# A two-layer fp32 decoder trunk: the seven-product results kept as one running sum in one PSUM bank, and two groups in every pair of the feed-forward's second part

## The chip, the cores and the metric

The kernel runs on one core of a Trainium2 chip. The metric is device time in microseconds (us) of one execution; less is better. Engines are named as in the profile: PE is TensorE (matmuls and transposes), PEld its weight loads, DVE is VectorE, ACT is ScalarE, POOL is GpSimd, SP the queue that issues most of the transfers.

## What is computed

Each of two layers runs a pre-normed mixer (a gated convolution branch beside forgetting attention), a SwiGLU feed-forward stage and a per-layer input embedding, all added onto x. There are 256 positions, 2048 model columns and 5632 hidden columns. The parts that the change touches are these products:

```
def rmsnorm(x, g):
    xf = x.astype(jnp.float32)
    y = xf * lax.rsqrt(jnp.mean(xf * xf, axis=-1, keepdims=True) + EPS)
    return (y * g.astype(jnp.float32)).astype(x.dtype)
...
    for i in range(DEPTH):
        h = rmsnorm(x, norm_mix_g[i])
        proj = h @ w_in[i]
        ...
        merged = jax.nn.sigmoid(g_conv) * y_conv + jax.nn.sigmoid(g_attn) * y_attn
        x = x + merged @ w_out[i]

        hf = rmsnorm(x, norm_ffn_g[i])
        gate, up = jnp.split(hf @ w_gate_up[i], 2, axis=-1)
        x = x + (jax.nn.silu(gate) * up) @ w_down[i]

        hp = rmsnorm(x, norm_ple_g[i])
        x = x + jax.nn.sigmoid(hp @ w_ple_gate[i]) * (p[i] @ w_ple_proj[i])
    return rmsnorm(x, final_g)
```

All weights are fp32, and every weight is read once from HBM.

## The kernel before

**Splits.** A weight piece is 128 partitions x 1024 numbers (two k-tiles of 128 rows, 512 columns each, 512 KB). `fetch` (L135) brings it on SP's queue into one of eight `raw` buffers. `split` (L138 to L144) makes two tensors of it that TensorE can take at full rate: `wh`, a rounded copy (ACT, L141), and `wl`, the rest `raw - wh` (DVE, L142), five buffers each. The operands on the activation side are split alike. A k-tile's product is then three matmuls of 512 columns, `xh*wh`, `xh*wl` and `xl*wh` (`Sum.add`, L184, L185, L186); a piece in the plain form is used for two blocks of 128 positions, so it takes 12 matmuls.

**The seven-product form.** `fast_chunks` (L233 to L310) makes two outputs of 512 columns, w1 and w2, over a list of groups of 512 rows of the weights. For the first groups, as many as `fast` holds, it takes the Strassen-Winograd form: the four quarter blocks of the pair of outputs come from seven products of six matmuls, 42 in place of 48. The operand side (B11 to N4X) is made once per group by `Fast.make` (L364 to L374): four small DVE sums on 128x256, then the splits (ACT L373, DVE L374). On the weight side a11, a12, a22 are pieces as fetched, and `sm` is w1 + w2, added while it lands by an accumulating transfer that POOL issues. Three DVE sums of 128x1024 per group (`add` L271, `sub` L272) make the other weight operands in place in the raw buffers. Before, four products add into banks of their own over all groups (`p1, q5, q6, q7`, tag ms, four banks of 512 columns in all, shared with the transposes), the other three straight into the output sums (tag mm). After the last group ACT copies p1 (L293) and DVE makes four sums of 128x512 with q6, q7 and twice q5 (L272, L271).

The remaining groups are plain: `go` fetches, splits and multiplies one piece. `u1` plus the first output's plain sum is the first result (`first(u1)`), `u2` is subtracted from the second output's plain sum at the end (the u2 subtraction, L272, whose operand is an mm bank).

**What sets the order.** Each engine has an in-order queue. A list scheduler puts the instructions into these queues, by data and by buffer dependences; the source order is what it starts from. Small work (transposes of finished operands, `turned` L334 with `halves` L321/L322 or `Fast.take`) hangs in a list and is released by `run()` calls between pieces. In a two-group call of `fast_chunks` before, `run()` is called only in the plain part that follows the groups; in a one-group call over eight plain tiles it is also called inside the group.

**Where it is called.** Twice two pairs for gates in the mixer, `w_out` (two pairs, one group in the first and two in the second), the feed-forward stage, and the per-layer embedding (PLE, one group in the first pair and two in the second). The feed-forward stage runs in three parts of 3, 4 and 4 hidden chunks (`FFN_PARTS`). A part first makes its hidden chunks, one gate/up pair per chunk c (operands `norm.fast`, L916 to L927: Silu on ACT, then two STT at L924 that multiply up by gate), then two pairs of the down product onto x (`residual` L881). The number of fast groups, nf, is 1 in the first pair of each and 2 in the others: `nf = 1 if c == c0 else 2` (gate/up), `nf = 1 if n == 0 else len(fast_hid)` (down). The PLE's pair ends in `embed` (sigmoid on ACT L963, two DVE instructions L965 and L966).

Of the kernel before, what the change touches and what calls it, by code (L numbers as in the profile page):

```python
# [13 lines left out]
ALU = mybir.AluOpType  # L14
# [31 lines left out]
def trunk(ctx, tc, xT, xR, pT, wI, wF, wC, wA, wOut, wGU, wD, wPG, wPP, vec, bF, gF, out):  # L46
# [124 lines left out]


    class Sum:
        def __init__(self, n, bank):
            self.n, self.left, self.bank = n, n, bank

        @property
        def t(self):
# [2 lines left out]
        def add(self, xh, xl, wh, wl):  # L181
            start = self.left == self.n
            self.left -= 1
            pe.matmul(self.t, lhsT=xh, rhs=wh, start=start, stop=False)  # L184
            pe.matmul(self.t, lhsT=xh, rhs=wl, start=False, stop=False)  # L185
            pe.matmul(self.t, lhsT=xl, rhs=wh, start=False, stop=self.left == 0)  # L186

    def once(make):

# [48 lines left out]
    def fast_chunks(fast, w1, w2, xs, ks, first, by_block=None):  # L238

        nf, nk = 2 * len(fast), 4 * len(ks)
        p1, q5, q6, q7 = (Sum(nf, once(bank_ms)) for _ in range(4))
        c1, c11, c12 = sums_of_blocks(nf + nk)
        c2, c21, c22 = sums_of_blocks(nf + nk, nk)
        if by_block is not None:
            c22 = Sum(nk, once(bank_ms))
        left = deque()
        for w, sums in ((w1, (c11, c12)), (w2, (c21, c22))):
            for g, k0 in enumerate(ks):  # L250
                for half in range(2):
                    left.append((w[len(fast) + g][:, half * 1024 : (half + 1) * 1024], sums, k0 + 2 * half))
        state = dict(quiet=True)

        def go(n=1):
            for _ in range(n):
                src, sums, k0 = left.popleft()
                parts = split(fetch(src))
                await_x(xs, (k0, k0 + 1))
                plain(sums, xs, k0, parts)  # L260
                if not state["quiet"]:
                    fill(CONV // 2 + len(left) % 2)
                    run()

        def product(to, operand, raw):
            h, l = split(raw)
            xh, xl = operand
            for kk in range(2):
                to.add(xh(kk), xl(kk), h[:, kk, :], l[:, kk, :])

        add = lambda o, a, b: dve.tensor_tensor(o, a, b, op=ALU.add)  # L271
        sub = lambda o, a, b: dve.tensor_tensor(o, a, b, op=ALU.subtract)  # L272
        u1, u2 = pair(), pair()
        for g, f in enumerate(fast):
            a11, sm = fetch(w1[g][:, :1024]), fetch(w2[g][:, :1024])
            nc.gpsimd.dma_start(sm.rearrange("p k n -> p (k n)"), w1[g][:, :1024], accum_op=ALU.add)
            a22, a12 = fetch(w2[g][:, 1024:]), fetch(w1[g][:, 1024:])
            product(p1, f(B11), a11)
            product(c21, f(N4X), a22)
            go()  # L280
            product(c11, f(B21), a12)
            if len(left) > 2 * len(ks):
                go()
            if nk == 8 and len(fast) == 1:
                run()
            product(q7, f(T3), sm)
            add(sm, sm, a22)
            product(q6, f(T2), sm)
            sub(a11, sm, a11)
            product(q5, f(M1), a11)  # L290
            add(a12, a12, sm)
            product(c12, f(B22), a12)
        act.activation(u1[:, 0, :], p1.t, AF.Copy)  # L293
        sub(u1[:, 1, :], u1[:, 0, :], q6.t)
        add(u2[:, 0, :], u1[:, 1, :], q7.t)
        add(u1[:, 1, :], u1[:, 1, :], q5.t)
        add(u2[:, 1, :], u2[:, 0, :], q5.t)
        state["quiet"] = False
        go(len(left) - 2 * len(ks))
        add(u1, u1, c1())  # L300
        first(u1)
        if by_block is None:
            go(len(left))
            sub(u2, c2(), u2)
            return u2
        go(len(left) - 4)
        held = [(split(fetch(src)), k0) for src, _, k0 in left]
        for b, c in enumerate((c21, c22)):
            for parts, k0 in held:
                plain([c, c], xs, k0, parts, [b])  # L310
            sub(u2[:, b, :], c.t, u2[:, b, :])
            by_block(b, u2)
# [25 lines left out]

        return (lambda b: o[:, b * P : (b + 1) * P]), (lambda b: o[:, S + b * P : S + (b + 1) * P])

    B11, B12, B21, B22, M1, T2, T3, N4X = range(8)

    class Fast:

# [17 lines left out]
        def make(self):  # L362
            f = lambda n: self.f[n // 4][:, n % 4]
            sub = lambda o, a, b, op: dve.tensor_tensor(f(o), f(a), f(b), op=op)  # L364
            sub(M1, B11, B12, ALU.subtract)
            sub(T2, M1, B22, ALU.add)
            sub(T3, B22, B12, ALU.subtract)
            sub(N4X, B21, T2, ALU.subtract)
            self.h, self.l = [], []
            for t in self.f:  # L370
                h, l = (pair(F32R).rearrange("p a b -> p (a b)") for _ in range(2))
                t = t.rearrange("p n k s -> p (n k s)")
                act.activation(h, t, AF.Copy)  # L373
                dve.tensor_tensor(l, t, h.bitcast(F32), op=ALU.subtract)  # L374
                self.h.append(h.rearrange("p (n k s) -> p n k s", n=4, k=2))
                self.l.append(l.rearrange("p (n k s) -> p n k s", n=4, k=2))
            self.f = None
# [167 lines left out]
    for i in range(L):  # L545
# [357 lines left out]
        for part, nch in enumerate(FFN_PARTS):  # L903
            hid = {}
            fast_hid = [Fast() for _ in range(nch - 2)]
            for c in range(c0, c0 + nch):
                w1, w2 = wGU[i, 2 * c], wGU[i, 2 * c + 1]
                o = pair() if c == 0 else None

                def gate(g):  # L910
                    nonlocal o
                    if o is None:
                        o = g
                    for b in range(2):
                        act.activation(o[:, b, :], g[:, b, :], AF.Silu, scale=norm.r(b))

                if c == 0:
                    gate(chunk(by_four(w1), norm.xs))
                    up = chunk(by_four(w2), norm.xs)
                else:  # L920
                    nf = 1 if c == c0 else 2
                    up = fast_chunks(norm.fast[:nf], w1, w2, norm.xs, range(4 * nf, KD, 4), gate)
                for b in range(2):
                    dve.scalar_tensor_tensor(  # L924
                        o[:, b, :], up[:, b, :], norm.r(b), o[:, b, :], op0=ALU.mult, op1=ALU.mult
                    )
                turns.append(  # L927
                    lambda c=c, o=o, hid=hid, fast=fast_hid[c - c0] if c - c0 < len(fast_hid) else None:
                    operand(hid, 4 * c, lambda b: o[:, b, :], fast)
                )  # L930
            for n in range(0, N4, 2):
                await_x(hid, (4 * c0,))
                on = after if part == len(FFN_PARTS) - 1 else None
                nf = 1 if n == 0 else len(fast_hid)
                onto_x(on, n + 1)(
                    fast_chunks(
                        fast_hid[:nf], wD[i, n][c0 : c0 + nch], wD[i, n + 1][c0 : c0 + nch], hid,
# [129 lines left out]
```

## Time and profile before

| | us |
|---|---|
| median of three runs (2793.18 to 2793.36) | 2793.24 |
| the profiled execution's own time | 2793.7 |
| its span | 2791.8 |

| engine | busy us | share of the span |
|---|---|---|
| PE | 2773.9 | 99% |
| PEld | 2293.5 | 82% |
| DVE | 2507.1 | 90% |
| ACT | 1660.0 | 59% |
| POOL | 79.4 | 3% |

The core moved 585.24 MB at 210 GB/s on average, and the granted clock was 0.999. The profile gives a row for each instruction with its start and its length. PE's rows overlap: a matmul's length is modelled and is longer than the distance to the next one, so what a matmul costs is read from the distance of two starts, and a real wait of PE shows as a greater distance. Rows of DVE overlap by some 80 ns too. "x8" behind a row says that eight equal ones follow each other; a name in brackets says who ended the idle time ahead of it.

### The profile page before, as it was taken

How to read it: one execution, taken by the hardware profiler on the slowest of the kernel's cores; microseconds unless marked ns; L12 is line 12 of the kernel's file. 1: busy time of each engine (PE TensorE's matmuls, PEld its weight loads, DVE VectorE, ACT ScalarE, POOL GpSimd, SP SyncE). 2: the span in 40 equal slices, each digit the busy share in tenths (PEclk: the TensorE clock that was granted, in tenths of full speed). 3: DMA queues.
4: the chain of work that ended last, by engine and by line, in shares of the span. 5: the costliest groups of instructions: out<-in, count | busy, mean ns of one | idle time of the engine just before them, and what ended most of it. 6: DMA issues, size and time to landing. Idle time of an engine off the chain costs nothing.

```text
span 2791.8 us, 34941 instructions
## 1 busy us (share of the span) xinstructions
PE 2773.9 (99%) x12568; PEld 2293.5 (82%) x12568; DVE 2507.1 (90%) x3003; ACT 1660.0 (59%) x2002; POOL 79.4 (3%) x121
## 2 busy tenths in 40 slices
PE   9999999999999999999999999999999999999998
PEld 7888888888888888888888888888888888888886
DVE  7999889888989988999979988988799899889998
ACT  7445766565556655656754466655665565556565
POOL 0000000000000000000000000000000000000000
PEclk9999999999999999999999999999999999999999
DMA  7555557666676766776655555575666677677674
GB/s 299 188 182 185 199 186 227 198 217 201 217 226 220 227 218 220 224 221 203 215 186 190 185 181 199 189 233 184 228 205 215 216 232 231 203 229 218 217 239 131
DMA packets 161597, 585.24 MB, mean 210 GB/s; under 512 B 18192, under 2 KB 18448, under 8 KB 161168
## 3 DMA queue, kind: packets, MB, share of 16 engines
q1 hardware_dynamic: 149040, 539.50, 56.5%
q0 software_dynamic: 11520, 41.95, 8.3%
q8 instruction: 98, 1.61, 0.2%
q10 hardware_dynamic: 864, 1.57, 0.2%
q14 instruction: 75, 0.61, 0.1%
HBM read 580.85 MB, written 2.10 MB: 209 GB/s over the span
## 4 chain that ended last, share of the span: by engine, by line
PE 93%; DVE 3%; issue 3%; ACT 1%; POOL 0%; POOLq 0%; ACTq 0%; DVEq 0%
PE mm L186 25%; PE mm L185 25%; PE mm L184 25%; PE ms L184 5%; PE ms L185 5%; PE ms L186 5%; PE ms L334 2%; DVE wl L142 1%; DVE raw L271 0%; PE ms L726 0%; ACT wh L141 0%; PE ms L755 0%; DVE pair L374 0%; PE ms L745 0%; DVE pair L271 0%
## 5 line engine op out<-in xcount | busy, mean ns | idle before, releaser
L141 ACT ACTIVATE wh<-raw 128x1024 fp32r<-128x1024 f32 x1254 | 1300.5, 1058 | 1022.7 <-PE mm L186 576.7
L142 DVE TENSOR_TENSOR wl<-raw,wh 128x1024 fp32r<-128x1024 f32 x1254 | 1501.0, 1219 | 212.4 <-ACT wh L141 204.9
L184 PE MATMUL mm<-wh,pair 128*128 128x512 f32 x3224 | 1261.9, 392 | 1.1 <-ACT pair L324 0.7
L185 PE MATMUL mm<-wl,pair 128*128 128x512 f32 x3224 | 1256.6, 390 | 0.9 <-DVE wl L142 0.8
L186 PE MATMUL mm<-wh,pair 128*128 128x512 f32 x3224 | 1256.8, 390 | 0.5 <-DVE pair L325 0.5
L186 PEld LDWEIGHTS mm<-wh,pair 128*128 128x128 f32 x3224 | 605.2, 188 | 128.4 <-DVE pair L325 1.4
L185 PEld LDWEIGHTS mm<-wl,pair 128*128 128x128 f32 x3224 | 605.6, 188 | 126.3 <-DVE wl L142 3.2
L184 PEld LDWEIGHTS mm<-wh,pair 128*128 128x128 f32 x3224 | 605.4, 188 | 126.0 <-ACT pair L324 1.7
L184 PE MATMUL ms<-wh,pair 128*128 128x512 f32 x680 | 265.7, 391 | 0.1
L186 PE MATMUL ms<-wh,pair 128*128 128x512 f32 x680 | 264.7, 389 | 0.0
L185 PE MATMUL ms<-wl,pair 128*128 128x512 f32 x680 | 264.6, 389 | 0.0
L569 DVE SCALAR_TENSOR_TENSOR pair<-pair,vecs,pair 128x256 f32<-128x256 f32 x480 | 201.1, 474 | 0.0
L271 DVE TENSOR_TENSOR raw<-raw,raw 128x1024 f32<-128x1024 f32 x160 | 195.4, 1222 | 2.6
L184 PEld LDWEIGHTS ms<-wh,pair 128*128 128x128 f32 x680 | 127.7, 188 | 28.0 <-ACT pair L998 0.9
L186 PEld LDWEIGHTS ms<-wh,pair 128*128 128x128 f32 x680 | 127.6, 188 | 26.7
L185 PEld LDWEIGHTS ms<-wl,pair 128*128 128x128 f32 x680 | 127.7, 188 | 26.0
L272 DVE TENSOR_TENSOR raw<-raw,raw 128x1024 f32<-128x1024 f32 x80 | 98.0, 1225 | 2.6
L271 DVE TENSOR_TENSOR pair<-pair,ms 128x512 f32<-128x512 f32 x144 | 93.9, 680 | 0.0
L272 DVE TENSOR_TENSOR pair<-mm,pair 128x1024 f32<-128x1024 f32 (+1 forms) x48 | 58.1, 1210 | 11.5 <-PE mm L186 11.4
L271 DVE TENSOR_TENSOR pair<-pair,mm 128x1024 f32<-128x1024 f32 x48 | 58.3, 1215 | 5.5 <-PE mm L186 5.5
L374 DVE TENSOR_TENSOR pair<-pair,pair 128x1024 fp32r<-128x1024 f32 x52 | 62.8, 1217 | 0.0
L373 ACT ACTIVATE pair<-pair 128x1024 fp32r<-128x1024 f32 x52 | 54.3, 1055 | 2.7 <-DVE pair L364 1.6
(168 smaller groups left out, 1065.0 us busy)
## 6 DMA issues: line engine op xcount, KB each, us to landing
raw<-in_wGU_dram SPq DMA_DIRECT2D x352, 512.0 KB, 4.8
raw<-in_wI_dram SPq DMA_DIRECT2D x287, 512.0 KB, 4.0
raw<-in_wD_dram SPq DMA_DIRECT2D x176, 512.0 KB, 4.8
raw<-in_wOut_dram SPq DMA_DIRECT2D x64, 512.0 KB, 4.6
raw<-in_wPG_dram SPq DMA_DIRECT2D x64, 512.0 KB, 4.9
raw<-in_wGU_dram POOLq DMA_DIRECT2D x36, 512.0 KB, 7.9
raw<-in_wA_dram SPq DMA_DIRECT2D x32, 512.0 KB, 4.7
raw<-in_wC_dram SPq DMA_DIRECT2D x32, 512.0 KB, 4.9
```

Source lines behind the costliest of these rows:

```text
L141: act.activation(h, raw, AF.Copy)
L142: dve.tensor_tensor(l, raw, h.bitcast(F32), op=ALU.subtract)
L184: pe.matmul(self.t, lhsT=xh, rhs=wh, start=start, stop=False)
L185: pe.matmul(self.t, lhsT=xh, rhs=wl, start=False, stop=False)
L186: pe.matmul(self.t, lhsT=xl, rhs=wh, start=False, stop=self.left == 0)
L271: add = lambda o, a, b: dve.tensor_tensor(o, a, b, op=ALU.add)
L272: sub = lambda o, a, b: dve.tensor_tensor(o, a, b, op=ALU.subtract)
L334: pe.transpose(pt[:, kk * S + b * P : kk * S + (b + 1) * P], src(b)[:, c : c + P], ident)
L373: act.activation(h, t, AF.Copy)
L374: dve.tensor_tensor(l, t, h.bitcast(F32), op=ALU.subtract)
L569: dve.scalar_tensor_tensor(cv[c], u[c][:, j : j + S], w, cv[c], op0=ALU.mult, op1=ALU.add,)
```

## The change

1. Three of the four small banks become one, `chain`. All groups' B11 products go in first and ACT copies the state to u1's first half; then the products with NT2, which is the negative of T2, and ACT copies the state to u1's second half; at the very end the T3 products, and ACT copies the state to u2's first half. `Sum` gets three stops. Only the two sums with q5 stay on DVE.
2. For this order `sm` of a group is fetched ahead and held to the end of the call, and all groups' a11 are fetched first. The sum sm + a22 is made in a22's buffer, the others follow from it.
3. In two-group calls with eight plain tiles `run()` is called inside the first group, as only one-group calls did.
4. `Fast.make` makes NT2 by one scalar_tensor_tensor (STT).
5. In the second feed-forward part the first gate/up pair and the first down pair take two fast groups in place of one: four more fast groups over the two layers.

```diff
-        p1, q5, q6, q7 = (Sum(nf, once(bank_ms)) for _ in range(4))
+        chain, q5 = Sum(3 * nf, once(bank_ms), 3), Sum(nf, once(bank_ms))
...
-        u1, u2 = pair(), pair()
+        def third(g):
+            sm = fetch(w2[g][:, :1024])
+            nc.gpsimd.dma_start(sm.rearrange("p k n -> p (k n)"), w1[g][:, :1024], accum_op=ALU.add)
+            return sm
+
+        s3 = [third(0)]
+        a11s = []
         for g, f in enumerate(fast):
-            a11, sm = fetch(w1[g][:, :1024]), fetch(w2[g][:, :1024])
-            nc.gpsimd.dma_start(sm.rearrange("p k n -> p (k n)"), w1[g][:, :1024], accum_op=ALU.add)
+            a11s.append(fetch(w1[g][:, :1024]))
+            product(chain, f(B11), a11s[g])
+        u1 = pair()
+        act.activation(u1[:, 0, :], chain.t, AF.Copy)
+        for g, f in enumerate(fast):
+            a11, sm = a11s[g], s3[g]
             a22, a12 = fetch(w2[g][:, 1024:]), fetch(w1[g][:, 1024:])
-            product(p1, f(B11), a11)
             product(c21, f(N4X), a22)
             go()
             product(c11, f(B21), a12)
             if len(left) > 2 * len(ks):
                 go()
-            if nk == 8 and len(fast) == 1:
+            if nk == 8 and g == 0:
                 run()
-            product(q7, f(T3), sm)
-            add(sm, sm, a22)
-            product(q6, f(T2), sm)
-            sub(a11, sm, a11)
+            if g < len(fast) - 1:
+                s3.append(third(g + 1))
+            add(a22, sm, a22)
+            product(chain, f(NT2), a22)
+            if g == len(fast) - 1:
+                act.activation(u1[:, 1, :], chain.t, AF.Copy)
+            sub(a11, a22, a11)
             product(q5, f(M1), a11)
-            add(a12, a12, sm)
+            add(a12, a12, a22)
             product(c12, f(B22), a12)
-        act.activation(u1[:, 0, :], p1.t, AF.Copy)
-        sub(u1[:, 1, :], u1[:, 0, :], q6.t)
-        add(u2[:, 0, :], u1[:, 1, :], q7.t)
+        for sm, f in zip(s3, fast):
+            product(chain, f(T3), sm)
         add(u1[:, 1, :], u1[:, 1, :], q5.t)
+        u2 = pair()
+        act.activation(u2[:, 0, :], chain.t, AF.Copy)
         add(u2[:, 1, :], u2[:, 0, :], q5.t)
...
-            sub(T2, M1, B22, ALU.add)
             sub(T3, B22, B12, ALU.subtract)
-            sub(N4X, B21, T2, ALU.subtract)
+            dve.scalar_tensor_tensor(f(NT2), f(M1), -1.0, f(B22), op0=ALU.mult, op1=ALU.subtract)
+            sub(N4X, B21, NT2, ALU.add)
...
-                    nf = 1 if c == c0 else 2
+                    nf = 1 if c == c0 and part != 1 else 2
...
-                nf = 1 if n == 0 else len(fast_hid)
+                nf = 1 if n == 0 and part != 1 else len(fast_hid)
```

In the changed program the lines lie further down: the u2 subtraction is L274, the sums L273, the STT of the feed-forward L939, `Fast.make` L379 to L389, the PLE's pair L980 and L981, the two ACT copies in the middle L286 and L302, the last one L311. By count of instructions PE has 24 fewer, DVE has 96 fewer sums of 128x512 with a small bank, 12 more sums and 12 more splits of 128x1024, ACT has 96 more copies of 128x512, 12 more of 128x1024 and 4 more table loads, POOL 4 more accumulating transfers.

How the rows move, first on DVE where the second part's gate/up pair for c = 5 begins in layer 0. Before, the u2 subtraction of the pair for c = 4 (the row with an mm bank) stands behind the four small sums and the two splits of `Fast.make`:

```order
L364 TENSOR_TENSOR pair_7367<-pair_7367,pair_7366 128x256
L142 TENSOR_TENSOR wl_7467<-raw_7451,wh_7466 128x1024
L364 TENSOR_TENSOR pair_7367<-pair_7366,pair_7367 128x256
L374 TENSOR_TENSOR pair_7380<-pair_7366,pair_7379 128x1024
L142 TENSOR_TENSOR wl_7480<-raw_7477,wh_7479 128x1024
L374 TENSOR_TENSOR pair_7384<-pair_7367,pair_7383 128x1024
L142 TENSOR_TENSOR wl_7497<-raw_7453,wh_7496 128x1024
L272 TENSOR_TENSOR pair_7092<-mm_7117,pair_7092 128x1024
L142 TENSOR_TENSOR wl_7509<-raw_7506,wh_7508 128x1024
L924 SCALAR_TENSOR_TENSOR pair_7091<-pair_7092,rt_5255,pair_7091 128x512 x2
```

At the same place of the changed program the subtraction stands ahead of them:

```order
L274 TENSOR_TENSOR pair_7349<-mm_7117,pair_7349 128x1024
L142 TENSOR_TENSOR wl_7495<-raw_7462,wh_7494 128x1024
L939 SCALAR_TENSOR_TENSOR pair_7107<-pair_7349,rt_5243,pair_7107 128x512 x2
L142 TENSOR_TENSOR wl_7507<-raw_7504,wh_7506 128x1024
L142 TENSOR_TENSOR wl_7553<-raw_7460,wh_7552 128x1024
L142 TENSOR_TENSOR wl_7564<-raw_7433,wh_7563 128x1024
L273 TENSOR_TENSOR raw_7462<-raw_7462,raw_7460 128x1024
L142 TENSOR_TENSOR wl_7576<-raw_7462,wh_7575 128x1024
L142 TENSOR_TENSOR wl_7590<-raw_7585,wh_7589 128x1024
L142 TENSOR_TENSOR wl_7602<-raw_7599,wh_7601 128x1024
L379 TENSOR_TENSOR pair_7528<-pair_7527 128x256 x2
L382 SCALAR_TENSOR_TENSOR pair_7528<-pair_7528,pair_7527 128x256
```

The subtraction has moved ahead, most of the pair's splits and `Fast.make` stand behind it, and one sum (raw_7462) is followed directly by the split of the same raw.

Second, on DVE where the PLE's second pair begins in layer 0; the rows with xt are the residual sum of the pair before. Before:

```order
L374 TENSOR_TENSOR pair_11242<-pair_11223,pair_11241 128x1024
L142 TENSOR_TENSOR wl_11441<-raw_11425,wh_11440 128x1024
L272 TENSOR_TENSOR pair_10988<-mm_11013,pair_10988 128x1024
L142 TENSOR_TENSOR wl_11454<-raw_11451,wh_11453 128x1024
L965 TENSOR_TENSOR pair_10988<-pair_10988,pair_10964 128x1024
L142 TENSOR_TENSOR wl_11471<-raw_11427,wh_11470 128x1024
L966 TENSOR_TENSOR xt<-xt,pair_10988 128x2x512
L142 TENSOR_TENSOR wl_11483<-raw_11480,wh_11482 128x1024
```

In the changed program:

```order
L389 TENSOR_TENSOR pair_11216<-pair_11197,pair_11215 128x1024
L142 TENSOR_TENSOR wl_11411<-raw_11408,wh_11410 128x1024
L274 TENSOR_TENSOR pair_11089<-mm_10989,pair_11089 128x1024
L142 TENSOR_TENSOR wl_11427<-raw_11422,wh_11426 128x1024
L273 TENSOR_TENSOR raw_11422<-raw_11392,raw_11422 128x1024
L980 TENSOR_TENSOR pair_11089<-pair_11089,pair_10940 128x1024
L142 TENSOR_TENSOR wl_11440<-raw_11437,wh_11439 128x1024
L981 TENSOR_TENSOR xt<-xt,pair_11089 128x2x512
L142 TENSOR_TENSOR wl_11457<-raw_11424,wh_11456 128x1024
```

A weight sum (raw_11422) now stands between the subtraction and the splits of the pieces that follow.

Third, on ACT in the changed program, a gate/up pair with two groups from the second copy out of the running sum on (ms_7790) to the third; raw_7781 and raw_7889 are the held sums:

```order
L141 ACTIVATE wh_8010<-raw_7928 128x1024
L141 ACTIVATE wh_8020<-raw_7781 128x1024
L141 ACTIVATE wh_8030<-raw_7889 128x1024
L302 ACTIVATE pair_7809<-ms_7790 128x512
L141 ACTIVATE wh_8049<-raw_8047 128x1024
L141 ACTIVATE wh_8067<-raw_8065 128x1024
L141 ACTIVATE wh_8085<-raw_8083 128x1024
L141 ACTIVATE wh_8103<-raw_8101 128x1024
L930 ACTIVATE pair_7809<-pair_7809,rt_5243 128x512
L311 ACTIVATE pair_8041<-ms_7790 128x512
```

The copies of the held sums (raw_7781 and raw_7889, for the T3 products) are queued ahead of the read of the running sum; behind it stand the splits of plain pieces.

More of the change, by code (lines that the diff above doesn't have):

```diff
@@ L173, in trunk, with __init__ @@
     class Sum:
-        def __init__(self, n, bank):
-            self.n, self.left, self.bank = n, n, bank
+        def __init__(self, n, bank, rests=1):
+            self.n, self.left, self.bank, self.rest = n, n, bank, n // rests
         @property
@@ L183, in add @@
             self.left -= 1
-            pe.matmul(self.t, lhsT=xh, rhs=wh, start=start, stop=False)
-            pe.matmul(self.t, lhsT=xh, rhs=wl, start=False, stop=False)
-            pe.matmul(self.t, lhsT=xl, rhs=wh, start=False, stop=self.left == 0)
+            kw = dict(skip_group_check=self.rest < self.n)
+            pe.matmul(self.t, lhsT=xh, rhs=wh, start=start, stop=False, **kw)
+            pe.matmul(self.t, lhsT=xh, rhs=wl, start=False, stop=False, **kw)
+            pe.matmul(self.t, lhsT=xl, rhs=wh, start=False, stop=self.left % self.rest == 0, **kw)
     def once(make):
@@ L339, in by_blocks @@
         return (lambda b: o[:, b * P : (b + 1) * P]), (lambda b: o[:, S + b * P : S + (b + 1) * P])
-    B11, B12, B21, B22, M1, T2, T3, N4X = range(8)
+    B11, B12, B21, B22, M1, NT2, T3, N4X = range(8)
     class Fast:
```

## The prediction

> **What bounds the kernel now.** I read the page first: busy time by engine, then the chain that ended last.
>
> ```profile
> PE 2773.9 (99%) x12568; PEld 2293.5 (82%) x12568; DVE 2507.1 (90%) x3003; ACT 1660.0 (59%) x2002; POOL 79.4 (3%) x121
> PE 93%; DVE 3%; issue 3%; ACT 1%; POOL 0%; POOLq 0%; ACTq 0%; DVEq 0%
> ```
>
> PE carries the chain, DVE is close behind with 90%, the others are far. Since PE's lengths are modelled, I take its cost from starts: this stretch of PE's timeline holds nothing but matmuls of 512 columns, and there are 54 distances between the first row and the last.
>
> ```profile
> 999.73 0.39 PE L185 MATMUL mm<-wl,pair 128*128 128x512 f32 x1
> ...
> 1011.97 0.39 PE L185 MATMUL ms<-wl,pair 128*128 128x512 f32 x1
> ```
>
> 12.24 us over 54 is 0.2268 us per matmul. Next the waits of PE; three of the seven rows, the others are of 1.2 us at most and lie in the start and the attention:
>
> ```profile
> PE mm L185 <- DVE wl L142: 0.8, 3, 0.5
> PE ms L334 <- DVE xt L881: 0.7, 2, 0.4
> ...
> PE mm L184 <- ACT wh L141: 0.3, 1, 0.3
> ```
>
> PE practically never waits, so a matmul less is worth its 0.2268 us as long as DVE and ACT keep ahead of it. Whether they do in the stretches that change is the real question. Two windows show it, the first a gate/up pair with two groups, the second one with one group:
>
> ```profile
> core 0: us, PE busy (x) PEld busy (x) DVE busy (x) ACT busy (x) POOL busy (x), PEclk, DMA share, GB/s
> 1132.40:1174.70 42.30, 42.30 (x192) 34.96 (x191) 41.99 (x43) 27.14 (x29) 1.70 (x2) 1.00 0.73 225
> 1043.00:1075.00 32.00, 32.00 (x143) 26.49 (x142) 26.57 (x26) 17.42 (x18) 0.84 (x1) 1.00 0.76 253
> ```
>
> With two groups DVE is busy for 41.99 of 42.30 us; with one group it has 17% over. So a pair with two groups is one in which DVE runs level with PE, and it eats the lead that the other pairs build up.
>
> **Part 1, the matmuls.** Four more groups in the seven-product form, each 42 matmuls for 48: 24 x 0.2268 = **-5.4 us**. PE is the bound, nothing hides this.
>
> **Part 2, waits that go.** In each layer PE waits where the first feed-forward part goes on to its down product, and where the last part's residual must be ready to be transposed:
>
> ```profile
> 738.24 0.40 PE L184 MATMUL mm<-wh,pair 128*128 128x512 f32 x1
> 738.79 0.50 PE L185 MATMUL mm<-wl,pair 128*128 128x512 f32 x1 [0.15 <-DVE wl L142]
> 739.12 0.39 PE L184 MATMUL ms<-wh,pair 128*128 128x512 f32 x1
> ...
> 1299.72 0.39 PE L184 MATMUL mm<-wh,pair 128*128 128x512 f32 x1
> 1300.46 1.09 PE L334 MATMUL ms<-ident,xt 128*128 128x128 f32 x8 [0.35 <-DVE xt L881]
> 1301.59 0.50 PE L185 MATMUL mm<-wl,pair 128*128 128x512 f32 x1
> ```
>
> The same eight transposes where nothing is late:
>
> ```profile
> 1116.23 0.40 PE L186 MATMUL mm<-wh,pair 128*128 128x512 f32 x1
> 1116.47 1.04 PE L334 MATMUL ms<-ident,pair 128*128 128x128 f32 x8
> 1117.26 0.47 PE L184 MATMUL mm<-wh,pair 128*128 128x512 f32 x1
> 1117.57 0.39 PE L185 MATMUL mm<-wl,pair 128*128 128x512 f32 x1
> ```
>
> The first wait is 0.55 - 0.23 = 0.32 and 0.33 - 0.23 = 0.10, together 0.42; the second is 0.74 - 0.24 = 0.50 ahead of the transposes and 1.13 - 0.79 = 0.34 behind them, 0.84. They come once in each layer: 2.5 us. In both the wait is on DVE, and DVE loses work ahead of both (below). I count **-2.5**; the gain is at least 0 and at most this. The transposes themselves cost 1117.57 - 1116.23 less two matmuls, 0.9 us.
>
> **Part 3, what DVE and ACT do in all.** These groups give the prices:
>
> ```profile
> L271 DVE TENSOR_TENSOR pair<-pair,ms 128x512 f32<-128x512 f32 x144 | 93.9, 680 | 0.0
> L142 DVE TENSOR_TENSOR wl<-raw,wh 128x1024 fp32r<-128x1024 f32 x1254 | 1501.0, 1219 | 212.4 <-ACT wh L141 204.9
> L293 ACT ACTIVATE pair<-ms 128x512 f32<-128x512 f32 x48 | 27.7, 578 | 0.0
> L364 DVE TENSOR_TENSOR pair<-pair,pair 128x256 f32<-128x256 f32 x52 | 21.7, 418 | 1.9 <-ACT pair L358 1.8
> L848 ACT ACT_TABLE_LOAD x6 | 7.7, 1283 | 0.1
> ```
>
> A DVE row overlaps the next by about 0.08 us, so a sum of 128x512 takes 0.60, one of 128x1024 1.14 and one of 128x256 0.34 of its queue. DVE: 96 x 0.60 = 57.6 less, 24 x 1.14 = 27.4 more (the extra groups), an STT for a small sum makes no difference: 30 us less of 2507. ACT: 96 x 0.578 + 12 x 1.06 (a copy for a split, by a row in part 4) + 4 x 1.283 = 73 us more of 1660, and it has 40% to spare. By busy time alone the change is safe; what counts is where in the queues it puts things.
>
> **Part 4, a new tight place in two-group pairs.** This is how the end of such a pair runs on DVE now:
>
> ```profile
> 1168.59 1.22 DVE L272 TENSOR_TENSOR pair<-mm,pair 128x1024 f32<-128x1024 f32 x1
> 1169.72 1.22 DVE L142 TENSOR_TENSOR wl<-raw,wh 128x1024 fp32r<-128x1024 f32 x1
> 1170.86 1.41 DVE L924 SCALAR_TENSOR_TENSOR pair<-pair,rt,pair 128x512 f32<-128x512 f32 x2
> 1172.18 1.22 DVE L142 TENSOR_TENSOR wl<-raw,wh 128x1024 fp32r<-128x1024 f32 x1
> 1173.44 1.23 DVE L271 TENSOR_TENSOR raw<-raw,raw 128x1024 f32<-128x1024 f32 x1
> ...
> 1175.85 1.23 DVE L142 TENSOR_TENSOR wl<-raw,wh 128x1024 fp32r<-128x1024 f32 x1
> ```
>
> ACT, from the end of the sum at 1174.67 on:
>
> ```profile
> 1174.75 1.06 ACT L141 ACTIVATE wh<-raw 128x1024 fp32r<-128x1024 f32 x1 [4.86 <-DVE raw L271]
> ```
>
> The u2 subtraction at 1168.59 can't begin before the last matmul of the pair before, and everything behind it is bound to that time. Before, `Fast.make` and about eight splits of the new pair were ahead of it; in the changed order they are behind. Count from the subtraction to the split that the first plain piece of w2 needs: 15 splits, 4 weight sums, the subtraction, two splits of `Fast.make` and the sum with the bank of w1, 23 rows of 1.14 = 26.2; the small sums 1.4, the STT pair 1.32 (1170.86 to 1172.18), one sum of 128x512 0.6: 29.5. Added to this is one place where a sum is followed at once by the split of its own raw: DVE has to stand until ACT's copy is through; between the sum of 1173.44 and the split of 1175.85 lie 2.41 us, 1.15 of them the sum's own: 1.26 (here another sum fills them). That makes 30.8 us. PE has 132 matmuls and eight transposes to do in that time (29.9 + 0.92 = 30.9). The bare sum thus comes out at the limit, 0.08 over it with the hand-over; a walk in which every split also waits for ACT in ACT's order gives 0.58. Such a pair is reached with DVE late where it follows other two-group pairs with `Fast.make` on hand: c = 4, 5, 8 and 9, eight in the two layers. I take 8 x 0.58 = **+4.6** (8 x 0.1 to 8 x 1.2). For the four second pairs with two groups and a residual behind them (`w_out`, last down) the same walk gives up to 0.7 each; with less behind the subtraction I take **+2.0** (0 to 2.8).
>
> What also hangs on it are the buffers. The second group's `go` fetches into the raw buffer of the first group's a11, free only 18 matmuls, 4.1 us, ahead of its use where there were 30.
>
> ```profile
> raw<-in_wGU_dram SPq DMA_DIRECT2D x352, 512.0 KB, 4.8
> raw<-in_wI_dram SPq DMA_DIRECT2D x287, 512.0 KB, 4.0
> ```
>
> The first row is the feed-forward's, 4.8 us from issue to landing, more than 4.1; the second, the mixer's, is 4.0. The stand of 1.26 comes at the same place and would hide some of it; I leave the cost in the range and make it a rival.
>
> **Part 5, the PLE's second pair in layer 0.** PE has no lead there now, it waits for ACT's `wh`:
>
> ```profile
> 1365.43 0.39 PE L184 MATMUL ms<-wh,pair 128*128 128x512 f32 x1
> 1366.13 0.50 PE L184 MATMUL mm<-wh,pair 128*128 128x512 f32 x1 [0.31 <-ACT wh L141]
> ```
>
> That is 0.70 - 0.23 = 0.47 of wait. In the changed order a weight sum of 1.14 stands ahead of the splits there, which the lead does not cover, and later splits come late by as much. I take **+1.5** (from -0.6, if the wait goes, to +2.6, two places with 1.14 each and the wait).
>
> **Part 6, the tail and the mixer.** At the end the last block's chain waits on DVE behind the scaling of the other block:
>
> ```profile
> 2781.82 0.88 DVE L988 TENSOR_SCALAR xt<-xt,rt 128x512 f32<-128x512 f32 x2 [0.47 <-POOL rt L448]
> 2782.62 0.68 DVE L966 TENSOR_TENSOR xt<-xt,pair 128x512 f32<-128x512 f32 x1
> ```
>
> The first of these two scalings now stands ahead of that block's subtraction too: **+0.5** (-0.5 to +1.5). In the mixer `run()` comes earlier and four table loads are added; each lies on ACT, which has room, so **0** (-1.5 to +1.5, the bound being one table load of 1.283 us on the path).
>
> **Part 7, reads of the running sum.** PE may write `chain` again only after ACT has read it. Between the B11 products and the first NT2 product lie at least 36 matmuls, 8 us; between the last NT2 product and T3 lie q5 and c12, 12 matmuls, 2.7 us. How soon a read follows is seen where the subtraction waits for PE now, first PE's row, then DVE's:
>
> ```profile
> 1346.30 0.39 PE L186 MATMUL mm<-wh,pair 128*128 128x512 f32 x1
> ```
>
> ```profile
> 1346.72 1.23 DVE L272 TENSOR_TENSOR pair<-mm,pair 128x1024 f32<-128x1024 f32 x1 [0.21 <-PE mm L186]
> ```
>
> The read starts 0.4 us after the last matmul's start and lasts 0.58, about 1.0 us; one copy of 1.06 ahead of it in ACT's queue still fits. Cost 0; the copy for the held sums is queued ahead of the read. Were it not covered, it would be up to 0.8 for each of 48 reads.
>
> [...]
>
> The sum: -5.4 - 2.5 + 4.6 + 2.0 + 1.5 + 0.5 = +0.7. From the execution's own 2793.7 that is 2794.4; the median of the runs, 2793.24, lies 0.46 lower, so **2793.9 us**.
>
> **The rivals.** A run of this kernel can tell some 0.2%, 5.6 us, from no change: faster means below 2787.7, slower above 2798.8.
>
> First, DVE keeps its lead everywhere: the 30 us that it loses are spread over the pairs, and the tight place stays at its bare sum. Then -5.4 - 2.5 + 8 x 0.1 + 0.5 = -6.6, 2786.6 us. For it speaks that PE waits no more than 0.42 us at any place of this form in the feed-forward now; against it, that the place has no lead left by the count of part 4.
>
> Second, slower: the late buffer. If the fetch into a11's buffer takes its median of 4.8 where 4.1 are there, DVE comes 0.7 later in the twelve tight pairs, and nothing makes it up before the next: +8.6 on the forecast, 2802.5 us. It decides as soon as landing takes over 4.1 us in those pairs and the stand of 1.26 us does not cover it. The DMA share of 0.73 in the window speaks for longer landings, the eight buffers against.
>
> Third, PE waits on ACT's read of `chain`, 48 x 0.8 = 38 us, 2832 us. It would take ACT to be more than 1.7 us late at that place throughout; ACT's 59% speaks against. That the change doesn't do what it says (no group more) would leave 2793 plus the new tight places, in the range.
>
> **How the numbers follow.** The forecast with its bounds, within 0.2%: 0.57. DVE ahead, first rival: 0.24. Late buffer: 0.16. Bank: 0.03. The first rival and what of the forecast's own spread lies below 2787.7 make 0.25 for faster; the second and third with what lies above 2798.8 make 0.20 for slower; 0.55 for no change. The range takes in the first rival and most of the way to the second: 2786.0 to 2801.0.
>
> **What would show it.** In the profile of after: 24 matmuls fewer at a distance of 0.227; no wait at the two places of part 2; waits of PE for `wl` (L142) of about 0.6 in the pairs c = 4, 5, 8, 9; a sum L273 followed by some 1.2 us of idle DVE; PE waiting in the PLE's second pair; no PE wait on the L302 copy. The forecast is wrong if PE's waits stay below 3 us in all (first rival) or if raw's landing ends DVE's and ACT's waits (second).

## The result and the profile after

The changed kernel is slower: 2837.22 us, the median of four runs (2830.59 to 2841.1), against 2793.21 for the kernel before; the ratio is 1.0156, with a 95% interval of 1.0143 to 1.0169. The forecast was 2793.9, and the measured time lies outside its range. From the page of the profiled execution (2837.52 us), the span, the busy time of each engine, and the chain that ended last:

```profile
span 2835.8 us, 35108 instructions
PE 2784.8 (98%) x12544; PEld 2288.9 (81%) x12544; DVE 2475.8 (87%) x2931; ACT 1710.4 (60%) x2114; POOL 82.3 (3%) x125
PE 73%; DVE 11%; DMA 6%; issue 6%; ACT 3%; POOL 0%; ACTq 0%; DVEq 0%; POOLq 0%; SPq 0%
```

PE has the 24 instructions less (12568 to 12544), DVE 31 us less to do, as forecast. But the chain that ended last, which was 93% PE, is now 73% PE, and DMA stands in it with 6%, where before it had no share. PE's waits, first from the profile after:

```profile
PE mm L187 <- DVE wl L142: 16.9, 28, 1.6
PE mm L186 <- DVE pair L274: 12.7, 6, 3.6
PE ms L187 <- DVE wl L142: 2.4, 8, 0.3
```

The second row is new: TensorE waits for the u2 subtraction, six times, up to 3.6 us. No row names a read of the running sum by ACT (L286, L302, L311). Summed over all rows of PE, what its start-to-start distances have above 0.2268 us has grown from 21.0 to 69.4 us: 24 more ahead of a matmul that waits for a `wl`, 13.7 more behind the subtraction, and most of the rest where no releaser is named, in the restart behind a wait (4.8 more in the five distances that follow one; behind the wait at 735.02 the first is 0.31) and in matmuls at a lower clock (4.5, see the end). 48.4 less the 5.4 of the 24 matmuls, and 1 in other places, are the 44.0 us of the span.

Why DVE is late is told by its own waits, after:

```profile
DVE wl L142 <- ACT wh L141: 261.2, 249, 3.9
DVE raw L273 <- DMA raw<-in_wD_dram: 12.1, 5, 3.7
DVE raw L273 <- DMA raw<-in_wGU_dram: 8.2, 7, 2.5
```

and before, where no weight sum waits for a transfer:

```profile
DVE wl L142 <- ACT wh L141: 204.9, 158, 4.0
```

In the changed kernel DVE waits 20 us for transfers ahead of weight sums. One such place lies where the first down pair of layer 0 begins. POOL issues the accumulating transfer that makes the sum of w1 and w2:

```profile
718.17 0.87 POOL L277 DMA_DIRECT2D raw<-in_wD_dram  x1 [28.65 <-DVE pair L273]
```

DVE in the same stretch:

```profile
721.78 2.35 DVE L142 TENSOR_TENSOR wl<-raw,wh 128x1024 fp32r<-128x1024 f32 x2
727.85 1.23 DVE L273 TENSOR_TENSOR raw<-raw,raw 128x1024 f32<-128x1024 f32 x1 [3.72 <-DMA raw<-in_wD_dram]
...
733.66 1.22 DVE L274 TENSOR_TENSOR pair<-mm,pair 128x1024 f32<-128x1024 f32 x1
```

and PE:

```profile
731.30 0.39 PE L188 MATMUL mm<-wh,pair 128*128 128x512 f32 x1
735.02 0.47 PE L186 MATMUL mm<-wh,pair 128*128 128x512 f32 x1 [3.33 <-DVE pair L274]
...
737.13 0.63 PE L187 MATMUL mm<-wl,pair 128*128 128x512 f32 x1
737.55 0.63 PE L188 MATMUL mm<-wh,pair 128*128 128x512 f32 x1
```

Read together: the raw buffer came free and was fetched into at 711.45, the piece landed at 717.38, the accumulating transfer was issued at 718.17 and landed at 727.76, 16.3 us after the buffer was free. DVE stood before its sum from 724.1 on. Behind it in the queue stood the u2 subtraction, which needs no transfer at all, and PE could not begin the next sum in that bank until it was through. Before, in the same pair, the sum was complete at 723.78 and first used at 728.01.

Set side by side, each of the 84 accumulating transfers with the DVE sum that uses it: in 14 the sum starts less than 0.2 us after the landing, so that the landing sets its time; before there is none. Of the plain pieces (fetched, with nothing added in flight) 62 are split on ACT less than 0.2 us after they land; before there are 4.

The program's buffer names, set beside the traces, show what sets these times. Of the fetches 99 in 100 are issued within 0.3 us after the last use of the piece that held the buffer before, so it is the buffers that hold the fetches back. A complete sum lay ready for 11.3 us (median) ahead of its first use before, and for 2.8 at the least; in the changed kernel it is 7.8 and 0.1.

### The profile page after: what moved, and what is told of

Same layout as the page of the kernel before. It is cut to its first block, busy times and chain, and to the rows that moved or that the text cites. A ratio compares the mean times of both kernels' runs of the same rounds, so it can differ in the third digit from the quotient of the medians.

```text
span 2835.8 us, 35108 instructions
## 1 busy us (share of the span) xinstructions
PE 2784.8 (98%) x12544; PEld 2288.9 (81%) x12544; DVE 2475.8 (87%) x2931; ACT 1710.4 (60%) x2114; POOL 82.3 (3%) x125
## 4 chain that ended last, share of the span: by engine, by line
PE 73%; DVE 11%; DMA 6%; issue 6%; ACT 3%; POOL 0%; ACTq 0%; DVEq 0%; POOLq 0%; SPq 0%
PE mm L187 20%; PE mm L188 20%; PE mm L186 20%; DVE wl L142 6%; PE ms L186 4%; PE ms L187 4%; DMA raw<-in_wGU_dram 4%; PE ms L188 4%; ACT wh L141 2%; DMA raw<-in_wD_dram 2%; PE ms L349 1%; DVE raw L273 1%; DVE pair L273 1%; DVE raw L274 1%; DVE pair L389 1%
## 5 line engine op out<-in xcount | busy, mean ns | idle before, releaser
L186 PE MATMUL mm<-wh,pair 128*128 128x512 f32 x3184 | 1247.5, 392 | 13.1 <-DVE pair L274 12.7
L188 PE MATMUL mm<-wh,pair 128*128 128x512 f32 x3184 | 1242.2, 390 | 0.6 <-DVE pair L340 0.5
L186 PEld LDWEIGHTS mm<-wh,pair 128*128 128x128 f32 x3184 | 598.9, 188 | 139.8 <-issue 11.3
L188 PEld LDWEIGHTS mm<-wh,pair 128*128 128x128 f32 x3184 | 598.7, 188 | 126.5 <-DVE pair L340 1.2
L187 PE MATMUL ms<-wl,pair 128*128 128x512 f32 x712 | 278.4, 391 | 2.4 <-DVE wl L142 2.4
L186 PE MATMUL ms<-wh,pair 128*128 128x512 f32 x712 | 279.8, 394 | 0.0
L188 PE MATMUL ms<-wh,pair 128*128 128x512 f32 x712 | 277.7, 390 | 0.0
L273 DVE TENSOR_TENSOR raw<-raw,raw 128x1024 f32<-128x1024 f32 x168 | 204.9, 1220 | 22.2 <-DMA raw<-in_wD_dram 12.1
L188 PEld LDWEIGHTS ms<-wh,pair 128*128 128x128 f32 x712 | 133.6, 188 | 28.0
L186 PEld LDWEIGHTS ms<-wh,pair 128*128 128x128 f32 x712 | 133.7, 188 | 27.4 <-ACT pair L1013 0.4
L274 DVE TENSOR_TENSOR raw<-raw,raw 128x1024 f32<-128x1024 f32 x84 | 102.6, 1221 | 1.5
L273 DVE TENSOR_TENSOR pair<-pair,ms 128x512 f32<-128x512 f32 x96 | 65.3, 680 | 7.8 <-PE ms L188 7.8
L389 DVE TENSOR_TENSOR pair<-pair,pair 128x1024 fp32r<-128x1024 f32 x52 | 63.0, 1217 | 0.0
L273 DVE TENSOR_TENSOR pair<-pair,mm 128x1024 f32<-128x1024 f32 x48 | 58.3, 1214 | 4.8 <-PE mm L188 4.8
L274 DVE TENSOR_TENSOR pair<-mm,pair 128x1024 f32<-128x1024 f32 (+1 forms) x48 | 58.0, 1208 | 4.3 <-PE mm L188 4.2
L277 POOL DMA_DIRECT2D raw<-in_wGU_dram x38 | 32.5, 856 | 841.7 <-DMA raw<-in_wGU_dram 432.2
```

Source lines behind the costliest of these rows:

```text
L186: pe.matmul(self.t, lhsT=xh, rhs=wh, start=start, stop=False, **kw)
L187: pe.matmul(self.t, lhsT=xh, rhs=wl, start=False, stop=False, **kw)
```

## The experiments

Theory A: the data come late, since eight raw buffers now also hold sums and a11 pieces. Theory B: the four extra groups. Theory C: PE waits for reads of the one bank. Theory D: DVE's queue itself is too long, as my forecast had it. Theories E and F came later. Each run is against the kernel before on the same chip; 2792.4 to 2793.2 us there.

**The running sum alone.**

```diff
-                    nf = 1 if c == c0 and part != 1 else 2
+                    nf = 1 if c == c0 else 2
-                nf = 1 if n == 0 and part != 1 else len(fast_hid)
+                nf = 1 if n == 0 else len(fast_hid)
```

> The running sum and its new order, without the four extra groups of the second feed-forward part (24 matmuls more than the changed kernel). Theory A, late data: the weight sum that a call needs first lands only when DVE already stands in front of it, because eight raw buffers now also hold sums and a11 pieces; 8 of the 14 late places lie in calls that this edit leaves alone, so most of the loss stays: 2810 to 2825 us. Theory B, the extra groups are the cause (DVE has no pair left in which to catch up): back to 2790 to 2798 us. Theory C, TensorE waits for the reads of the one bank: the reads stay, so 2830 us or more.

2837.32 us (ratio 1.0160, 1.0145 to 1.0175), the same as with the extra groups. B is out. A's range was missed as well, the loss is not smaller at all: the 24 matmuls more cost nothing, because PE waits less by as much (its excess is 64.0 us instead of 69.4). C's number came true as well; against C stands that no row of PE names a read of the bank, and the third run.

**A short accumulation.**

```diff
-            nc.gpsimd.dma_start(sm.rearrange("p k n -> p (k n)"), w1[g][:, :1024], accum_op=ALU.add)
+            nc.gpsimd.dma_start(sm.rearrange("p k n -> p (k n)")[:, :64], w1[g][:, :64], accum_op=ALU.add)
```

> The changed kernel, order of all engines the same, but the accumulating transfer adds only 64 of the 1024 columns of each sum (the rest of w1's part of the sum is left out), so that a sum is complete several us earlier. Theory A1, the accumulating transfer's length is what makes the sum late: DVE no longer waits for it, the u2 subtraction behind it comes in time, TensorE's waits on L274 (13.7 us) and the lowered clock after them go: 2812 to 2818 us, or less if the splits' waits go too. Theory A2, the buffers make plain fetches late as well: the waits for the wl splits (26 us) stay. Theory D, DVE's queue itself is too long: 2835 us, no change.

This run leaves out most of w1's part of each sum, so it shows time alone. 2806.91 us (1.0057, 1.0042 to 1.0072). No wait on the subtraction is left; the waits for splits are about halved:

```profile
PE mm L187 <- DVE wl L142: 8.9, 16, 1.6
PE ms L187 <- DVE wl L142: 2.2, 8, 0.3
```

With the order of all queues kept, shorter transfers for the sums take away 30 of the 44 us. Not all of this is the sums' own landing: less is moved, and some 40 plain pieces are late instead of 62. D is out for those 30, C too, since all reads of the bank are as they were.

**Ten raw buffers.**

```diff
-PAIRS = 28
+PAIRS = 26
-RAWS = 8
+RAWS = 10
```

> The changed kernel with ten raw buffers instead of eight, paid with two of the 28 pair buffers; DVE's order differs in a handful of rows, PE's and ACT's not at all. Theory A, data comes late since buffers come free late: sums and plain pieces are fetched earlier, both kinds of wait go, 2788 to 2800 us. Theory D, DVE's queue is too long by itself (the dependent split behind a sum, the subtraction ahead of the splits): 2830 us or more. Theory C, reads of the bank: 2835 us.

2794.73 us (1.0008, 0.9999 to 1.0017), no loss that can be told. No sum is late any more (11.8 us ready in the median, 3.5 at the least), and 2 plain pieces instead of 62. PE's waits:

```profile
PE mm L187 <- DVE wl L142: 7.0, 15, 1.6
```

This is A: the same instructions in the same order on PE and ACT, six differing rows on DVE, and the 42 us are gone.

**Without the early release of transposes in two-group calls.**

```diff
-            if nk == 8 and g == 0:
+            if nk == 8 and len(fast) == 1:
                 run()
```

> The changed kernel without the early release of transposes in two-group calls. Theory A: the data are as late as before, 2830 to 2840 us. Rival: the early transposes put ACT and DVE work for the operands into the tight stretch and cause the waits there; then 2815 us or less.

2794.46 us (1.0008, 0.9999 to 1.0018). The expectation of A was a miss: with eight buffers the loss goes as well. The gate/up pair for c = 5 shows why, first DVE in the changed kernel, then in this one:

```profile
878.02 1.23 DVE L142 TENSOR_TENSOR wl<-raw,wh 128x1024 fp32r<-128x1024 f32 x1 [0.44 <-ACT wh L141]
880.55 1.23 DVE L273 TENSOR_TENSOR raw<-raw,raw 128x1024 f32<-128x1024 f32 x1 [1.30 <-DMA raw<-in_wGU_dram]
```

```profile
866.68 0.75 DVE L379 TENSOR_TENSOR pair<-pair 128x256 f32<-128x256 f32 x2
867.35 0.42 DVE L382 SCALAR_TENSOR_TENSOR pair<-pair,pair 128x256 f32<-128x256 f32 x1
867.68 1.22 DVE L389 TENSOR_TENSOR pair<-pair,pair 128x1024 fp32r<-128x1024 f32 x1
...
870.37 1.23 DVE L389 TENSOR_TENSOR pair<-pair,pair 128x1024 fp32r<-128x1024 f32 x1
871.51 1.22 DVE L273 TENSOR_TENSOR raw<-raw,raw 128x1024 f32<-128x1024 f32 x1
```

Here `Fast.make` stands ahead of the sum and the sum does not wait: its transfer landed at 868.20, 3.3 us before it starts. With the early release that work is gone from there, DVE arrives too soon and stands, and meets the same work later, between splits. Four sums are late instead of 14; 54 plain pieces still are, but PE waits only 4.4 us for splits and 2.4 for the subtraction, as DVE has kept its lead.

**The sum behind the subtraction and Fast.make.** Two instructions are held to the order of the program.

```diff
-            sub(u2, c2(), u2)
+            tc.keep_in_program_order(sub(u2, c2(), u2))
...
-            add(a22, sm, a22)
+            tc.keep_in_program_order(add(a22, sm, a22))
```

> The changed kernel with DVE held to the order in which the program is written for two of its instructions, the u2 subtraction and the first weight sum of the next call (with a22): both the subtraction and Fast.make then stand ahead of the sum in DVE's queue. Fetches, buffers and the early release of transposes stay. Theory E, order: the scheduler put a sum that waits for a late transfer ahead of work that is ready; with ready work ahead of it the waits go: 2790 to 2802 us. Theory A, the buffers alone: the sums land as late as before and DVE stands for them as long: 2825 us or more.

3077.44 us (1.1017, 1.1000 to 1.1034), which neither theory expected. The edit put all of `Fast.make` ahead of the sum, and that work needs the transposes that PE does just before it needs the sum:

```profile
PE ms L186 <- ACT wh L141: 163.3, 56, 7.0
```

It says nothing on E; a better edit follows.

**Ten buffers and no early release, in one.**

> The changed kernel without the early release in two-group calls and with ten raw buffers (26 pair buffers). If what is left in each of the two alone is late data, the two add up: 2786 to 2790 us, faster than the kernel before. If what is left is DVE's own length in the two-group pairs, as my forecast had it: 2792 to 2795 us.

2785.76 us (0.9975, 0.9965 to 0.9985): faster than both kernels, and just beyond the range of the two added up. What PE still waits for splits:

```profile
PE mm L187 <- DVE wl L142: 2.7, 3, 1.6
```

**The running sum alone, without early release.**

> The running sum alone: no early release, no extra groups, eight raw buffers. If the extra groups are worth their 24 matmuls, this is 5.4 us slower than with them (2794.5): 2799 to 2801 us. If DVE is the bound where they are made, they gain less: 2794 to 2797 us.

2800.49 us (1.0029, 1.0018 to 1.0039), against 2794.46 with the extra groups: without the early release they are worth 6.0 us, their 24 matmuls and half a microsecond. It also shows that the running sum by itself, with its order and eight buffers, costs 8 us; five waits for the subtraction, 6.1 us in starts, are in it.

**Ten buffers in the kernel before.**

> The kernel before with ten raw buffers and 26 pair buffers. If late data are a matter of the changed kernel alone, nothing moves: 2791 to 2794 us. If more buffers help any kernel of this form: 2788 us or less.

2792.61 us (1.0000, 0.9991 to 1.0009). The kernel before does not miss buffers, and two pair buffers fewer cost nothing.

**The sum later on DVE.** The sum of the first group is written ahead of the early release and held there, with the subtraction ahead of it. On DVE both, and four splits, then stand ahead of the sum, and `Fast.make` behind it.

```diff
+            if g == 0:
+                tc.keep_in_program_order(add(a22, sm, a22))
             if nk == 8 and g == 0:
                 run()
...
-            add(a22, sm, a22)
+            if g > 0:
+                add(a22, sm, a22)
...
-            sub(u2, c2(), u2)
+            tc.keep_in_program_order(sub(u2, c2(), u2))
```

> The changed kernel with the first weight sum of a call (sm + a22) written ahead of the early release and held, with the u2 subtraction, to the order of the program: on DVE the sum then stands behind the subtraction and behind four splits instead of ahead of them, and ahead of Fast.make. Fetches, eight buffers and the early release stay. Theory E, order: DVE comes to the sum some 5 us later, when it has landed, and nothing that is ready stands behind it: 2792 to 2802 us, no TensorE wait on L274. Theory A, buffers alone: the sums are as late for TensorE as before, so 2825 us or more.

2820.01 us (1.0098, 1.0084 to 1.0111). Between the two expectations: no sum is late, and of the waits for the subtraction 0.6 us are left; but 91 plain pieces are, and PE waits about as long for splits as in the changed kernel:

```profile
PE mm L187 <- DVE wl L142: 17.7, 30, 2.4
PE mm L186 <- DVE pair L274: 0.6, 2, 0.3
```

So with eight buffers moving the sum takes 17 us off the 44. The next run takes 19 more off with ten buffers and leaves 8, so this order has a price of its own.

**The same with ten buffers.**

> The same with ten raw buffers and 26 pair buffers. If both act on the same lateness, this is no better than the better of the two alone (2792 to 2796 us); if plain pieces are still late with eight buffers, 2785 to 2790 us.

2800.66 us (1.0029, 1.0018 to 1.0041). A miss: worse by 6 than ten buffers alone. With data in time, the scheduler's order was the better one. (Here the scheduler ordered some rows otherwise than in the run before, so the 19 us are not of the buffers alone.)

**Nine buffers.**

> The changed kernel with nine raw buffers and 27 pair buffers: half the dose of the run with ten. Theory A: the data come about 2 us earlier per buffer and the waits at the sums were at most 3.7 us, so most of the loss is gone with one buffer: 2796 to 2808 us. If it takes both buffers: 2815 us or more.

2795.15 us (1.0009, 1.0000 to 1.0018). One buffer does all that two do. Three sums are still late, nine plain pieces:

```profile
DVE raw L273 <- DMA raw<-in_wD_dram: 2.0, 2, 1.4
```

**A faster version with more groups.** To the sixth run (no early release, ten buffers), two groups in the first pairs of the third part as well:

```diff
-                    nf = 1 if c == c0 and part != 1 else 2
+                    nf = 1 if c == c0 and part == 0 else 2
-                nf = 1 if n == 0 and part != 1 else len(fast_hid)
+                nf = 1 if n == 0 and part == 0 else len(fast_hid)
```

> The version without the early release and with ten raw buffers (2785.8 us), with two groups also in the first pairs of the third part: 24 matmuls fewer, 5.4 us. If DVE keeps its lead: 2779 to 2782 us. If the two-group pairs in a row use it up: 2784 to 2790 us.

2781.93 us (0.9961, 0.9948 to 0.9975), 3.8 us less than without. It is the fastest of all runs.

**Fast.make put off, the transposes early.**

```diff
+    put_off = [False]
...
-                self.make()
+                turns.append(self.make) if put_off[0] else self.make()
...
             if nk == 8 and g == 0:
+                put_off[0] = len(fast) == 2
                 run()
+                put_off[0] = False
```

> The changed kernel with the early release of transposes kept, but Fast.make (four small sums and two splits on DVE, 5.1 us) of a group that is transposed there put off to the next release, in the plain part. Theory F: what the early release costs is Fast.make in the middle of the tight two-group stretch, where DVE should be splitting pieces as they land; then 2790 to 2802 us, about as without the early release. Rival: the eight transposes on PE and their copies on ACT at that place are what costs; then 2825 us or more.

2813.32 us (1.0079, 1.0062 to 1.0096), between the two. In the gate/up pairs of the second and third part the waits are all but gone, so `Fast.make` in the two-group stretch is what costs there; putting it off is worth 24 us in all. (By the rows of the run without early release it is 4.0 us of DVE per group, not the 5.1 of the expectation.) What stays are mostly sums in down pairs, where PE again waits for the subtraction (4.2, 2.9, 3.9 and 3.0 us between starts in four of them). DVE's waits for these sums, whose line is L274 in this kernel:

```profile
DVE raw L274 <- DMA raw<-in_wD_dram: 11.7, 6, 3.4
```

How much of these 19 us is the transposes' and copies' own time, and how much the order that the scheduler gave to this edit, is open.

## Why the forecast was wrong, point by point

**The step that failed** is the last paragraph of part 4, on the buffers. It looked at one transfer only, the second group's `go`, put its cost into the range and kept 0 in the sum. That transfer did come late: some 25 of the 62 late plain pieces went into a buffer that had held an a11. But it was not the only one, and the transfer that held DVE longest was another: the sum of w1 and w2, which needs two transfers in a row, 14 to 16.5 us from a free buffer to a complete sum in the 14 late places, and which the new order needs earlier: DVE's sum with a22 is now its first use, where it was ACT's copy for the T3 product. The page of before has a row for these accumulating transfers,

```profile
raw<-in_wGU_dram POOLq DMA_DIRECT2D x36, 512.0 KB, 7.9
```

7.9 us on top of the 4.8 of the fetch that they wait for; the forecast worked out no lead for them. What the runs showed in place of the 0: late data, without which (ten buffers, PE's and ACT's order as it was) 42 of the 44 us are gone.

**The rivals.** The first, DVE ahead everywhere, was to show in PE's waits staying below 3 us in all; even with ten buffers those for splits alone are 7.0. The 2785.8 us of the run with ten buffers and no early release lie near its 2786.6 by another way and don't bear it out. The second, late buffers, had the right cause and side. It allowed 0.7 us in twelve pairs, 8.6 us; measured are 42. Three things were missing in it: that the sums are late as well as the plain pieces; that a waiting sum holds the u2 subtraction, and with it PE (13.7 us); and that the two longest waits, 3.33 and 3.59 us of idle, cost clock on top (4.5 us, see the end). The third, reads of the one bank, gave a time near the measured one (2832) by a mechanism that is not there: no wait of PE names these reads, and with ten buffers they cost nothing. A number that fits is no proof of its mechanism. Here the 12 matmuls between the last NT2 product and the first T3 product were enough: in the profile after, each of the 48 reads at L302 is through 0.28 us or more ahead of that product (1.92 in the median), and no run shows a cost.

**Part 1**, the matmuls: 24 fewer, worth 6.0 us without the early release and 0.1 with it and eight buffers, where PE only waits longer.

**Part 2**, the waits that go: both are gone with ten buffers. In the changed kernel the first came back as the 3.3 us wait at 735.02.

**Part 3**, the busy time: DVE has 31 us less, 30 were counted; ACT has 50 more, 73 were counted. ACT is at 60% and nothing hung on it.

**Part 4**, the tight place. With ten buffers it can be seen by itself, and it is what was worked out: one wait of 0.52 to 0.58 us (0.58 forecast) in each of the eight gate/up pairs c = 4, 5, 8, 9, for example

```profile
905.11 0.50 PE L187 MATMUL mm<-wl,pair 128*128 128x512 f32 x1 [0.36 <-DVE wl L142]
```

(0.53 above a matmul's distance), and one of 0.48 to 0.50 (0.5 taken) in each of the four second pairs of `w_out` and the last down product.

**Part 5**, the PLE's second pair: with ten buffers

```profile
1351.98 0.50 PE L187 MATMUL mm<-wl,pair 128*128 128x512 f32 x1 [1.60 <-DVE wl L142]
1360.63 0.50 PE L187 MATMUL mm<-wl,pair 128*128 128x512 f32 x1 [0.60 <-DVE wl L142]
```

1.83 and 0.76 us above a matmul's distance, less the 0.47 that went: +2.1 where I took +1.5.

**Part 6** took the early release as a matter of the mixer: 0, and with ten buffers two waits came there, 0.68 us between starts where 0.11 is usual. That the early release also works in the feed-forward's two-group calls, and moves `Fast.make` from a place where DVE had time to one where it had none, stood in the order (part 4 counts it), but the forecast took it as half a microsecond per pair. The tail gave nothing: from PE's last start to the end it is 13.1 us before and 12.8 with ten buffers.

**It takes two things together to make the loss.** Four runs side by side: 2837.2 us with eight buffers and the early release, 2794.7 with ten buffers, 2794.5 without the early release, 2785.8 with ten buffers and without it. So the early release costs 9 us where data are on time and 43 where they are late; two buffers are worth 9 us without it and 42 with it. Either one taken away brings the change level with the kernel before; both taken away make it 6.8 us faster.

So the forecast holds, within 1 to 2 us, for a kernel whose data are on time (2793.9 against 2794.7 and 2795.2 measured), and the assumption that they are was not checked. That is no chance hit: as measured with ten buffers the terms come to -5.4 - 2.5 + 4.3 + 2.0 + 2.1 + 1.1 - 0.3 = +1.3 us, where +0.7 was forecast; the spans of the two profiles differ by 1.0, the medians of the runs by 2.3.

## What to carry to other kernels

When an edit moves the first use of a piece of data, or keeps buffers for longer, work out for each transfer, and for each pair of transfers that follow each other, the time from the buffer's release to the first use, and compare it with issue to landing, before costing the engines. DVE takes its queue in order: the sum of 727.85, which waited 3.72 us for its transfer, held all that stood behind it, so look for what is ready there. A buffer more is the cheapest test of this.

## What the runs showed of the hardware

Two TensorE waits of the changed kernel cost more than their length. After the wait of 3.72 us between starts at 735.02 the matmuls' distance went from 0.227 to 0.427 us (737.13 to 737.55 above) for some eight of them. The granted clock of this stretch, of the one behind it, and of the other layer's:

```profile
736.50:739.90 3.40, 3.40 (x10) 2.61 (x10) 3.10 (x4) 0.35 (x1) 0.00 (x0) 0.54 0.48 169
739.90:745.00 5.10, 5.10 (x28) 4.34 (x27) 2.63 (x3) 3.04 (x4) 0.00 (x0) 1.00 0.90 291
2143.30:2149.50 6.20, 6.12 (x15) 4.86 (x16) 4.66 (x5) 0.57 (x1) 0.00 (x0) 0.51 0.46 153
```

The granted clock is the column ahead of the last two: 0.54 and 0.51, then 1.00 again. A wait in the third part's down product, 3.37 us between starts, was followed by matmuls at a granted clock of 1.00 (1226.0 to 1231.5), 0.30 us behind the first and 0.22 to 0.24 from then on:

```profile
1226.25 0.39 PE L188 MATMUL mm<-wh,pair 128*128 128x512 f32 x1
1229.62 0.47 PE L186 MATMUL mm<-wh,pair 128*128 128x512 f32 x1 [2.97 <-DVE pair L274]
1229.92 0.40 PE L187 MATMUL mm<-wl,pair 128*128 128x512 f32 x1
```

By the trace PE was idle for 3.33 us ahead of the first, for 3.59 in the other layer and for 2.97 ahead of this last one. The clock fell behind the two longer of these waits and not behind the shortest; what decides that, no run shows. The first of the two was followed by 4.65 us of matmuls until they were at 0.227 us again (735.02 to 739.67), the one in the other layer by 6.05 (2143.38 to 2149.43). The matmuls at the lower clock took about 4.5 us more than at the full one, over the two layers.

What the splits gain shows in the profile before. Among the products there of plain fp32 operands is L794, with 256 columns. It begins at 355.14 and stands as two rows; with one rounded matmul of 512 columns behind it, it takes until 355.81, 0.67 us, and 0.44 without that matmul's 0.227: about twice the time for half the columns.
